# Row norms of a two-layer hybrid diffusion block: 32-column sums of squares, an earlier context norm, a scale built during attention

## The chip, the cores and the metric

The kernel runs on one core of a Trainium2 chip. The metric is the device time of one execution in microseconds (us), lower is better. The engines are named as in the profile: PE (TensorE matmuls) and PEld (its weight loads), DVE (VectorE), ACT (ScalarE), POOL (GpSimd), SP (the queue that issues the DMAs).

## The reference, cut to what matters

Two layers over 512 latent tokens and 256 context tokens, width 1024. Layer 0 is multi-head latent attention, layer 1 a Hyena convolution; each is followed by a gated ConvFFN, and a last RMSNorm ends the program. Every sub-layer starts with a modulated RMSNorm:

```python
def rmsnorm(x, g):
    y = xf * lax.rsqrt(jnp.mean(xf * xf, axis=-1, keepdims=True) + EPS)
    return y * g

mod_x = silu(c) @ mod_w[i] + mod_b[i]          # six vectors of 1024
sh1, sc1, g1, sh2, sc2, g2 = split(mod_x, 6)
hx = rmsnorm(x, norm_mix_g[i]) * (1 + sc1) + sh1
x = x + g1 * mixer(hx)
x = x + g2 * conv_ffn(rmsnorm(x, norm_ffn_g[i]) * (1 + sc2) + sh2)
```

The attention also normalises the 512 query latents (g_q) and the 256 key and value latents (g_kv). Context tokens pass through the same first norm, with their own modulation vector c_ctx, and feed keys and values.

## The kernel before, in words

Activations lie transposed: 128 partitions hold one of 8 chunks of the model width (NC), tokens run along the free axis (T = 512, TC = 256 for the context). Each product is three PE matmuls on a high and a low part (`mm3`, L144); every matmul is recorded on L68. `split_w` (L130) loads a weight block into `wr`, ACT casts it to `wh` (L137), DVE subtracts to `wl` (L138); there are two `wh` and two `wl` buffers.

The stages in order:

- **Filter stage** (`filter_phase`, L383, about 0 to 74 us). Position features give the Hyena filters. In each half `hf`, a loop over four token tiles makes two products `fps`; DVE windows them into `ff` (L439, two buffers), ACT casts to `pqh` (L440), and `pql` is the difference (L441: on POOL for a = 0, on DVE for a = 1). Four small transforms per half follow (`fa`, `fb`, `fo`), whose results DVE combines into `fev` and `fs`. Between the steps `between()` (L506) pops a list of hooks: the modulation rows of layer 0 (`Mods.step_pe`), the squares of x (`nm.add`) and weight splits.
- **Latents** (`latents`, L538, to about 160 us). x is normalised and modulated into `hx` (L314 to L316), products `kv` follow, then the context norm (`rstd_bc`, L306, ordered after the last `hx`), its `ch`/`cl`, the `dq` products, the norm of the key and value latents (`nk`, called halfway through the second `dq` block by `norm_kv`, L570) and that of the query latents (`nq`).
- **Attention** (`attention`, L654, to about 376 us). Eight pairs of heads; each pair has twelve steps, and `side(n, i)` (L848) weaves the next pair's work into step i. Sums of the exponentials go through DRAM (`rst`) and come back as the broadcast `rb`; `normalize` (L813) uses it.
- **Projection and FFN of layer 0** (`project`, L900, to 424 us; `ffn`, L924, to 810 us), then Hyena (to 1020 us), a second projection and FFN, and the final norm.

**A norm** (`Norm`, L240). `add` squares a chunk; all but the last are summed on POOL into `sqa` (L275), the last is squared on DVE into `sq` (L280). `colsum` (L253) then sums over partitions on PE: for each 128 tokens a matmul with the squares as 128x128 stationary operand and one column of ones, so the sums lie along partitions, one column for 128 tokens. `finish` (L284) takes the reciprocal root in eleven DVE instructions on these 2, 4 or 6 columns (L291 to L298), spreads each column over the identity (`dg`, L301) and multiplies by ones into `bc`, the root broadcast over partitions. Norms around `project` and `ffn` work in two token halves (`halves=2`); the first half's `finish` is issued by `mid` in the middle of the last block.

**The scale and shift of FFN 0.** Group (0, 4) of the modulation (1024 columns) is accumulated during `project` by `Mods.step` (L214): eight DMAs of 512 KB and eight DVE instructions into `macc` (L225, L227), then `modp` (ones times `macc`), a copy `ev`, transposes `modq` and the bias add into `modc`; `make_gs` (L236) makes the gain `gsc` that `hx` multiplies by. Group (0, 5) and layer 1's follow inside `ffn`.

The order of instructions on each engine is fixed when the kernel is built, by a scheduler that goes by program order and by when it reckons operands ready, so that work can run ahead of its place in the source (the context's squares, written in `latents`, run at 50 us). `in_order` forces an order of two instructions without a wait.

Of the kernel before, what the change touches and what calls it, by code (L numbers as in the profile page):

```python
# [17 lines left out]
P = 128  # L18
# [29 lines left out]
CST = [("ident", 128), ("perm", 128), ("tneg", 4), ("sgn", 1)]  # L48
# [5 lines left out]
NCST = _o  # L54


@with_exitstack
def hybrid_kernel(ctx, tc, A, out):
# [8 lines left out]
    def mm(*args, **kw):  # L67
        i = nc.tensor.matmul(*args, **kw)  # L68
        in_order(lane["after"], i)
        if lane["since"] is not None:  # L70
            lane["since"].append(i)
        return i
# [24 lines left out]
    cst = gp.tile([P, NCST], F32, name="cst")  # L97
    dma(out=cst, in_=A["cst"])
# [14 lines left out]
    nc.vector.tensor_copy(out=perm_r, in_=K("perm"))  # L113
    ones = gp.tile([P, P], F32, name="ones")
    nc.gpsimd.memset(ones, 1.0)
    modc = gp.tile([P, 2, 48, 2], F32, name="modc")
    gsc = gp.tile([P, 5, 8], F32, name="gsc")
    hcc = gp.tile([P, 3, 24], F32, name="hcc")
    sc = gp.tile([P, 8, 32], F32, name="sc")
    nc.gpsimd.memset(sc, 0.0)  # L120
    act(out=sc[:, :, 0], in_=V("c"), func=AF.Silu)
    act(out=sc[:, :, 1], in_=V("cctx"), func=AF.Silu)
# [36 lines left out]
    class Mods:  # L159
# [11 lines left out]
        def rows(self, lhsT, w, n, first, last):  # L171
            if first:
                self.p = psum[0].tile([P, 512], F32, tag="m", name="modp", bufs=1)
            c = n * 256
            for g in range(4):
                in_order(self.gate, mm(self.p[32 * g:32 * g + 32, :c], lhsT=lhsT, rhs=w[:, g * c:(g + 1) * c], start=first, stop=last))
# [14 lines left out]
        def step_pe(self, n, ws, pool, ahead=0):  # L191
            for _ in range(min(n, len(self.todo))):
                l, u, n, k = self.todo.pop(0)
                self.rows(sc[:, k, :], ws.pop(0), n, k == 0, k == NC - 1)
                if k == NC - 1:
                    self.columns(l, u, n, 2, pool)
                if ahead and len(self.todo) >= ahead:
                    ws.append(self.load(self.todo[ahead - 1], pool, "mw", ahead))

# [14 lines left out]
        def step(self, n, pool, bufs, after):  # L214
# [4 lines left out]
            for _ in range(min(n, len(self.todo))):  # L219
# [3 lines left out]
                if k == 0:  # L223
                    self.acc = pool.tile([P, 2048], F32, tag="macc", name="macc", bufs=2)[:, :n * 1024]
                    i = vts(out=self.acc, in0=w, scalar1=sc[:, k, 0:1], scalar2=None, op0=ALU.mult)  # L225
                else:
                    i = stt(out=self.acc, in0=w, scalar=sc[:, k, 0:1], in1=self.acc, op0=ALU.mult, op1=ALU.add)  # L227
# [12 lines left out]
    class Norm:  # L240
# [7 lines left out]

        def flush(self, lag=0):
# [3 lines left out]
        def colsum(self, src, h, first, last):  # L253
            for t in range(self.nth):
                m = mm(self.cols[h][:, t:t + 1], lhsT=src[:, t * P:(t + 1) * P], rhs=ones[:, 0:1],
                       start=first and t == 0, stop=last and t == self.nth - 1)
                self.last[h] = in_order(self.last[h], m)

        def add(self, xj, h=None):
            self.n_add += 1  # L260
            self.flush(self.nh)
# [9 lines left out]
            sq = self.tmp.tile([P, self.nt * P], F32, tag="sq", name="sq", bufs=2)[:, :w * len(hs)]  # L271
# [12 lines left out]
        def finish(self, bc, h=0, after=None, mm_after=None):  # L284
# [3 lines left out]
            nt, tmp = self.nth, self.tmp  # L288
            v = tmp.tile([P, 3, 8], F32, tag="rsq", name="rsq", bufs=2)
            vv, y, t_ = v[:, 0, :nt], v[:, 1, :nt], v[:, 2, :nt]  # L290
            in_order(after, vts(out=vv, in0=self.cols[h][:, :nt], scalar1=1.0 / self.dim, scalar2=EPS, op0=ALU.mult,  # L291
# [44 lines left out]
    class ToH:  # L336
# [7 lines left out]
        def prep(self, mm_after=None):  # L344
            i = len(self.bc)
            self.bc.append(pso("bc")[:, :self.n])
            self.nm.finish([self.bc[i]], i, None, mm_after)
# [35 lines left out]
    def filter_phase(early, between, mods):  # L383
        with tc.tile_pool(name="fp", bufs=1, side="left", reuse_waits="tile") as fp:
# [42 lines left out]
            for hf in range(2):  # L427
# [3 lines left out]
                for t in range(4):  # L431
                    win = fp.tile([P, 512], F32, tag="win", name="win", bufs=2)
                    act(out=win, in_=dec[:, cs], func=AF.Exp, scale=K("tneg")[:, t:t + 1])
                    for a in range(2):
# [6 lines left out]
                        (vtt if a else nc.gpsimd.tensor_tensor)(out=pq[a][1][:, t, :], in0=f, in1=pq[a][0][:, t, :],  # L441
# [34 lines left out]
    def mla():  # L476
        L = {}
        with ExitStack() as st:
            a1 = st.enter_context(tc.tile_pool(name="a1", bufs=1, side="left"))
            x = a1.tile([P, NC, T], F32, tag="x", name="x")  # L480
            xc = a1.tile([P, NC, TC], F32, tag="xc", name="xc")
            psum_pool(st, "pa", 5)
# [12 lines left out]
            def first_loads():  # L495
# [4 lines left out]
                dma(out=xc, in_=A["ctx"])  # L500

            nm = Norm(NC, 4, D, a1)
            hooks, started, wk = [], [], []
            L["wdkv"] = wk

            def between():  # L506
                if not started:
# [3 lines left out]
                    add = lambda j: (lambda: nm.add(x[:, j, :]))  # L511
                    hooks.extend([()] * 2 + [(step, add(0), add(1))] + [(step, add(j)) for j in range(2, 8)] + [(step, ahead)])
                    hooks[HK] += (lambda: wk.append(split_w(A["wdkv0"], 2048)),)
# [17 lines left out]
            with tc.tile_pool(name="a2", bufs=1, side="left", reuse_waits="tile") as a2:  # L531
                latents(lambda n: mods.step_pe(n, ws, a1, 2), nm, a1, a1, a2, x, xc, L)
# [5 lines left out]
    def latents(step, nm, nrm, a1, a2, x, xc, L):  # L538
# [15 lines left out]
        for rh, rl, n, o in ((hh, hl, T, TC), (ch, cl, TC, 0)):  # L554
# [12 lines left out]
            step(2)  # L567
        nk = Norm(2, 6, 256, nrm)
# [9 lines left out]
        for b in range(2):  # L578
# [40 lines left out]
        kb = L["kb"]  # L619
# [34 lines left out]
    def attention(ab, L):  # L654
# [122 lines left out]
        def value_block(p, kts, sums=None):  # L777
# [20 lines left out]
            if sums is not None:  # L798
# [5 lines left out]
                rs = ab.tile([16, 64], F32, tag="rs", name="rs", bufs=1)  # L804
# [41 lines left out]
        half, parts = {}, []  # L846

# [463 lines left out]
```

## Time and profile before

| | |
|---|---|
| median of 3 runs | 1442.45 us (1441.16 to 1444.59) |
| the profiled execution's own time | 1443.6 us |
| its span in the profile | 1441.8 us |
| PE busy | 1377.4 us (96%) |
| DVE / ACT / POOL busy | 959.4 / 562.4 / 224.9 us |
| mean granted TensorE clock | 0.989 of full speed |

A row of the timeline is: start us, duration us, engine, line, operation, out<-in, shape, count, and in brackets the idle time of the engine before it and what ended it. Merged instructions share a row (x8). f32 matmuls appear as two records each. PEclk is the granted clock as a share of 2.4 GHz. Matmul ends are modelled, so spacing between starts tells more than durations.

### The profile page before, as it was taken

Reading aid. Unit: us, or ns where it says so; the run is one execution under the profiler, and the core shown is the slowest. Engines: PE = TensorE matmul, PEld = TensorE weight load, DVE = VectorE, ACT = ScalarE, POOL = GpSimd, SP = SyncE. Lnnn points to the kernel's source line nnn. Section 1 sums busy time; section 2 is a strip of 40 time slices with the busy share of each in tenths; the row PEclk is TensorE's granted clock in tenths of the full one; section 3 lists DMA queues with packets and bytes.
Section 4 is the critical chain, followed back from the end, with each engine's and each line's share of the span. In section 5 each row is a group of like instructions: output and inputs, shape, how many; then the busy total and the mean of one; then the engine's idle time right before and its main releaser. Section 6 shows DMA issues by size and latency. Waiting matters only on the chain. (4 is left out here: it accounts for less than half of the span.)

```text
span 1441.8 us, 17267 instructions
## 1 busy us (share of the span) xinstructions
PE 1377.4 (96%) x6702; PEld 1088.7 (76%) x6702; DVE 959.4 (67%) x1496; ACT 562.4 (39%) x856; POOL 224.9 (16%) x188
## 2 busy tenths in 40 slices
PE   5899899999989999999999999999999999999997
PEld 2577666665679788787878988787798888888886
DVE  6875766577378777567764788888776553455545
ACT  5434545556335433133432343232344331234320
POOL 3401055354230000000001011332300000000011
PEclk9999999999999999999999999999999999999999
DMA  9672411114362645655513432222313223322121
GB/s 372 220 260 111 139 48 56 44 57 150 106 224 90 240 157 190 244 213 175 183 64 129 172 125 88 97 79 88 128 52 114 83 77 114 113 96 79 60 81 59
DMA packets 46670, 186.58 MB, mean 129 GB/s; under 512 B 5320, under 2 KB 17864, under 8 KB 32380
## 3 DMA queue, kind: packets, MB, share of 16 engines
q1 hardware_dynamic: 46588, 185.48, 37.3%
q8 instruction: 52, 0.85, 0.2%
q14 instruction: 30, 0.25, 0.0%
HBM read 171.29 MB, written 11.60 MB: 127 GB/s over the span
## 5 line engine op out<-in xcount | busy, mean ns | idle before, releaser
L137 ACT CAST wh<-wr 128x1024 fp32r<-128x1024 f32 (+1 forms) x203 | 190.0, 958 | 185.6 <-PE dn L68 89.0
L138 DVE TENSOR_TENSOR wl<-wr,wh 128x1024 fp32r<-128x1024 f32 (+1 forms) x203 | 238.1, 1189 | 18.1 <-ACT wh L137 15.6
L275 POOL TENSOR_TENSOR sqa<-sqa,sq 128x512 f32<-128x512 f32 (+1 forms) x42 | 57.2, 1362 | 844.7 <-ACT sq L273 843.9
L68 PE MATMUL dn<-gh,wl 128*128 128x512 f32 (+1 forms) x396 | 146.7, 370 | 0.0
L68 PE MATMUL dn<-gh,wh 128*128 128x512 f32 (+1 forms) x396 | 146.6, 371 | 0.0
L68 PE MATMUL dn<-gl,wh 128*128 128x512 f32 (+1 forms) x396 | 146.5, 370 | 0.0
L326 DVE SCALAR_TENSOR_TENSOR z<-ua,vec,z 128x511 f32<-128x511 f32 x44 | 33.0, 750 | 111.6 <-ACT z L325 111.5
L970 DVE SCALAR_TENSOR_TENSOR x<-dn,modc,x 128x512 f32<-128x512 f32 (+1 forms) x36 | 24.9, 691 | 109.4 <-PE dn L68 109.4
L325 ACT ACTIVATE z<-ua,vec 128x512 f32<-128x512 f32 x44 | 34.3, 779 | 150.8 <-PE ua L68 150.8
L68 PEld LDWEIGHTS dn<-gh,wh 128*128 128x128 f32 x396 | 74.3, 188 | 15.8 <-ACT wh L137 0.8
L68 PEld LDWEIGHTS dn<-gl,wh 128*128 128x128 f32 x396 | 74.4, 188 | 14.1
L68 PEld LDWEIGHTS dn<-gh,wl 128*128 128x128 f32 x396 | 74.5, 188 | 13.9
L771 POOL TENSOR_TENSOR acc<-acc,pf 128x512 f32<-128x512 f32 x60 | 77.6, 1315 | 26.6 <-ACT pf L761 25.9
L68 PE MATMUL hz<-hyh,wh 128*128 128x512 f32 (+1 forms) x224 | 81.5, 365 | 0.0
L68 PE MATMUL hz<-hyh,wl 128*128 128x512 f32 (+1 forms) x224 | 81.4, 364 | 0.0
L68 PE MATMUL hz<-hyl,wh 128*128 128x512 f32 (+1 forms) x224 | 81.1, 363 | 0.0
L761 ACT ACTIVATE pf<-s 128x512 f32<-128x512 f32 x96 | 57.3, 597 | 45.4 <-PE s L68 42.8
L68 PE MATMUL ua<-hf1h,wh 128*128 128x512 f32 (+1 forms) x192 | 72.9, 380 | 1.1 <-ACT hf1h L315 1.1
L68 PE MATMUL ua<-hf0h,wh 128*128 128x512 f32 (+1 forms) x192 | 73.3, 382 | 0.0
L68 PE MATMUL ua<-hf1l,wh 128*128 128x512 f32 (+1 forms) x192 | 72.8, 379 | 0.5 <-DVE hf1l L316 0.5
L68 PE MATMUL ug<-hf1h,wl 128*128 128x512 f32 (+1 forms) x192 | 73.0, 380 | 0.0
L68 PE MATMUL ua<-hf0l,wh 128*128 128x512 f32 (+1 forms) x192 | 72.9, 380 | 0.0
(382 smaller groups left out, 3383.8 us busy)
## 6 DMA issues: line engine op xcount, KB each, us to landing
wr<-in_wup SPq DMA_DIRECT2D x44, 1024.0 KB
mw<-in_modw SPq DMA_DIRECT2D x40, 1024.0 KB
wr<-in_wdn SPq DMA_DIRECT2D x32, 704.0 KB
wr<-in_win SPq DMA_DIRECT2D x12, 1024.0 KB
mw<-in_modw SPq DMA_DIRECT2D x16, 512.0 KB
fspec<-fs SPq DMA_DIRECT2D x16, 256.0 KB
wr<-in_wo SPq DMA_DIRECT2D x4, 1024.0 KB
fq<-fspec SPq DMA_DIRECT2D x8, 512.0 KB
```

The source lines that it names most:

```text
L68: i = nc.tensor.matmul(*args, **kw)
L137: nc.scalar.copy(out=wh[:, c], in_=wr[:, c])
L138: vtt(out=wl[:, c], in0=wr[:, c], in1=wh[:, c], op=ALU.subtract)
L275: nc.gpsimd.tensor_tensor(out=acc, in0=acc, in1=sq, op=ALU.add)
L325: act(out=z, in_=p, func=AF.Identity, bias=b, scale=w1)
L326: stt(out=z[:, 1:T], in0=p[:, 0:T - 1], scalar=w0, in1=z[:, 1:T], op0=ALU.mult, op1=ALU.add)
L761: act(out=pf, in_=s, func=AF.Exp, scale=ATT_SCALE)
L771: add(out=accs[h], in0=prev, in1=pf, op=ALU.add)
L970: i = stt(out=x[:, q, c], in0=job[0][:, c], scalar=mcol(l, 5, q), in1=x[:, q, c], op0=ALU.mult, op1=ALU.add)
```

## The change

- `colsum` now makes four matmuls with 32 columns of ones as stationary operand and the squares as moving operand, 32*nth tokens each (nth is a half's number of 128-token groups), into four bands of 32 partitions. Each band holds its sums in 32 equal rows. For norms of at most four token groups the sums are issued only in `roots`, the new first part of `finish`.
- The eleven root instructions then work on 128 x (32*nth) elements: 64, 128 or 192 columns. `dg` is gone. The broadcast is four matmuls whose stationary operand `pick` (built once for each pool on POOL) selects one row of a band.
- The roots of x run in a hook of the filter stage; the squares and roots of the context norm move to hooks behind them. In the filter's second half `pql` for a = 1 moves from DVE to POOL.
- `nk` keeps its squares in two tiles; its sums are flushed right after it is filled.
- Group (0, 4) leaves `project`: in attention, pairs 1 to 6, `mod_step` takes a 128x512 slice (16 DMAs of 256 KB into the free `vsb` buffers, 16 DVE instructions), and `mod_rows`/`mod_cols` turn the two halves into `modc` at pairs 4 and 7. `make_gs` then stands before `project`.
- The constant `perm` is loaded later, into a `sq` buffer, and cast on POOL; the exponent-sum tile `rs` shares a tile with `sm`.

```diff
         def colsum(self, src, h, first, last):
-            for t in range(self.nth):
-                m = mm(self.cols[h][:, t:t + 1], lhsT=src[:, t * P:(t + 1) * P], rhs=ones[:, 0:1],
-                       start=first and t == 0, stop=last and t == self.nth - 1)
+            w = self.nth * 32
+            for g in range(4):
+                q = src[g // 2][:, g % 2 * w:(g % 2 + 1) * w] if isinstance(src, list) else src[:, g * w:(g + 1) * w]
+                m = mm(self.cols[h][32 * g:32 * g + 32, :w], lhsT=ones[:, 0:32], rhs=q,
+                       start=first, stop=last)
                 self.last[h] = in_order(self.last[h], m)
...
         def add(self, xj, h=None):
             self.n_add += 1
-            self.flush(self.nh)
+            if self.nt > 4:
+                self.flush(self.nh)
...
-        def finish(self, bc, h=0, after=None, mm_after=None):
+        def roots(self, h=0, after=None, mm_after=None):
...
-            dg = tmp.tile([P, self.nt * P], F32, tag="sq", name="dg", bufs=2)
-            for t in range(nt):
-                vts(out=dg[:, t * P:(t + 1) * P], in0=ident, scalar1=y[:, t:t + 1], scalar2=None, op0=ALU.mult)
-            n = nt * P // len(bc)
-            for i, b in enumerate(bc):
-                in_order(mm_after, mm(b, lhsT=ones, rhs=dg[:, i * n:(i + 1) * n], start=True, stop=True))
+            return y
+
+        def finish(self, bc, h=0, after=None, mm_after=None, y=None):
+            if y is None:
+                y = self.roots(h, after, mm_after)
+            w = self.nth * 32
+            n = 4 // len(bc)
+            for g in range(4):
+                b = bc[g // n][:, (g % n) * w:(g % n + 1) * w]
+                in_order(mm_after, mm(b, lhsT=pick[0][:, g, :], rhs=y, start=True, stop=True))
...
-                        (vtt if a else nc.gpsimd.tensor_tensor)(out=pq[a][1][:, t, :], in0=f, in1=pq[a][0][:, t, :],
+                        (vtt if a and not hf else nc.gpsimd.tensor_tensor)(out=pq[a][1][:, t, :], in0=f, in1=pq[a][0][:, t, :],
                                                             op=ALU.subtract)
...
+                    hooks.append((lambda: L.update(yx=nm.roots(0, None, lane["last"])),))
+                    hooks.extend((lambda j=j: add_ctx(j),) for j in (0, 4))
+                    hooks.extend([(), (), (lambda: L.update(yc=nm_ctx[0].roots(0, None, lane["last"])),)])
...
         to_x = ToH(x, nm, 0, 0, 0, a2, "hx")
+        to_x.prep(None, L["yx"])
         step(2)
         hh, hl = to_x.run()
         bcc = pso("bcc")
-        rstd_bc([xc[:, j, :] for j in range(NC)], 2, D, nrm, [bcc[:, :TC]], to_x.end)
+        nm_ctx.finish([bcc[:, :TC]], 0, None, None, L["yc"])
...
                 for j in range(2):
                     nk.add(ckv[:, j, :])
+                nk.flush()
...
+                    if p and i in (1, 5, 9) and (mod["step"] != NC or p > 3):
+                        mod_step()
+                    if (p, i) in ((4, 0), (7, 0)):
+                        mod_rows(p // 7)
+                    if (p, i) in ((4, 2), (7, 2)):
+                        mod_cols(p // 7)
...
-        mods = Mods([(0, 4, 1)])
+        make_gs(2, 0, 4, "gffn0")
         th = ToH(x, Norm(NC, 4, D, fp, 2), 2, 0, 3, fp, "hf0")
-        project(x, oh, ol, "wo", 0, th.nm, lambda m: (mods.finish(), th.prep(m)), lambda i: mods.step(4, fp, 2, i) if mods.todo else mods.flush())
-        mods.finish()
-        make_gs(2, 0, 4, "gffn0")
+        project(x, oh, ol, "wo", 0, th.nm, th.prep, lambda i: None)
```

## Rows read from the trace of the kernel before

**Rows 1.** The page, part 1: busy time, share of the span, instructions.
```profile
PE 1377.4 (96%) x6702; PEld 1088.7 (76%) x6702; DVE 959.4 (67%) x1496; ACT 562.4 (39%) x856; POOL 224.9 (16%) x188
```

**Rows 2.** Windows: us, PE, PEld, DVE, ACT, POOL busy, PEclk, DMA share, GB/s.
```profile
50.00:60.00 10.00, 7.36 (x32) 5.12 (x30) 7.73 (x21) 4.54 (x12) 4.89 (x6) 1.00 0.35 110
60.00:70.00 10.00, 7.45 (x19) 5.60 (x20) 9.08 (x13) 4.46 (x7) 3.16 (x3) 0.66 0.70 274
```

**Rows 3.** Timeline of the filter's second half.
```profile
54.32 1.28 POOL L441 TENSOR_TENSOR pql<-ff,pqh 128x512 fp32r<-128x512 f32 x1 [1.44 <-ACT pqh L440]
...
59.28 0.72 ACT L273 ACTIVATE sq<-xc 128x256 f32<-128x256 f32 x2 [0.83 <-POOL sqa L275]
...
61.51 1.73 POOL L441 TENSOR_TENSOR pql<-ff,pqh 128x512 fp32r<-128x512 f32 x1
...
63.29 0.79 PE L68 MATMUL fo<-pql,dfto0h 128*128 128x512 f32 x1 [1.99 <-POOL pql L441]
```

**Rows 4.** Timeline of PE in the kv products.
```profile
87.21 0.70 PE L68 MATMUL bcc<-dg,ones 128*128 128x256 f32 x2 [0.78 <-DVE dg L301]
```

**Rows 5.** Timeline of PE in the second dq block.
```profile
127.63 1.39 PE L68 MATMUL cols<-ones,sq 128*128 128x1 f32 x12
...
128.88 0.47 PE L68 MATMUL dq<-hxh,wh 128*128 128x512 f32 x1
...
132.98 1.56 PE L68 MATMUL bk<-dg,ones 128*128 128x384 f32 x4 [1.05 <-DVE dg L301]
```

**Rows 6.** Timeline from the last matmul of project to the first output of FFN 0.
```profile
423.69 0.28 PE L68 MATMUL pj<-oh,wl 128*128 128x256 f32 x1
...
425.84 0.64 PE L68 MATMUL modp<-macc,ones 128*32 128x256 f32 x8 [1.87 <-DVE macc L227]
...
450.31 0.78 ACT L325 ACTIVATE z<-ua,vec 128x512 f32<-128x512 f32 x1 [3.23 <-PE ua L68]
```

**Rows 7.** The same two ends at FFN 1, which has no modulation work.
```profile
1051.65 0.28 PE L68 MATMUL pj<-yh,wl 128*128 128x256 f32 x1
...
1073.52 0.78 ACT L325 ACTIVATE z<-ua,vec 128x512 f32<-128x512 f32 x1 [2.40 <-PE ua L68]
```

**Rows 8.** Timeline of PE, first half of the final norm, inside a running stream.
```profile
1421.81 0.50 PE L68 MATMUL cols<-ones,sqa 128*128 128x1 f32 x4
...
1422.62 0.37 PE L68 MATMUL dn<-gh,wh 128*128 128x256 f32 x1
...
1425.57 0.70 PE L68 MATMUL bc<-dg,ones 128*128 128x256 f32 x2 [0.18 <-DVE dg L301]
1425.91 0.47 PE L68 MATMUL dn<-gh,wh 128*128 128x256 f32 x1
```

**Rows 9.** Lines of DVE by form: busy us, mean ns of one, idle before.
```profile
L314 DVE SCALAR_TENSOR_TENSOR hx<-x,gsc,bc 128x256 f32<-128x256 f32 x48 | 21.7, 476 | 3.8 <-PE bc L68 3.7
...
L301 DVE TENSOR_SCALAR dg<-cst,rsq 128x128 f32<-128x128 f32 x32 | 7.3, 282 | 0.6
...
L296 DVE SCALAR_TENSOR_TENSOR rsq<-rsq 128x2 f32<-128x2 f32 x27 | 4.3, 158 | 0.6
```

**Rows 10.** PE around one 32-column burst in the filter stage (timeline).
```profile
29.75 0.39 PE L68 MATMUL fa<-pql,dfteh 128*128 128x512 f32 x1
29.98 0.40 PE L68 MATMUL fa<-pqh,dftel 128*128 128x512 f32 x1
30.31 1.07 PE L68 MATMUL modp<-mw,sc 128*32 128x512 f32 x8
31.30 0.49 PE L68 MATMUL fb<-pqh,dfteh 128*128 128x512 f32 x1
```

**Rows 11.** Attention: one window, PE's waits (total, times, longest), the macc group.
```profile
200.00:300.00 100.00, 96.73 (x454) 64.81 (x452) 64.39 (x114) 57.51 (x102) 49.31 (x38) 1.00 0.18 54
...
PE mr L68 <- DVE mx L742: 4.3, 6, 1.0
...
L227 DVE SCALAR_TENSOR_TENSOR macc<-mw,sc,macc 128x1024 f32<-128x1024 f32 x14 | 20.8, 1487 | 0.8 <-DMA mw<-in_modw 0.7
```

More of the change, by code (lines that the diff above doesn't have):

```diff
@@ L54 @@
 NCST = _o
+NCP = COFF["perm"][0]
 @with_exitstack
@@ L68, in mm, with tr @@
         i = nc.tensor.matmul(*args, **kw)
+        in_order(lane["after"], i)
+        if lane["since"] is not None:
+            lane["since"].append(i)
+        lane["last"] = i
+        return i
+    def tr(**kw):
+        i = nc.tensor.transpose(**kw)
         in_order(lane["after"], i)
@@ L112, in hybrid_kernel, with make_pick @@
     nc.vector.tensor_copy(out=ident_r, in_=ident)
-    nc.vector.tensor_copy(out=perm_r, in_=K("perm"))
-    ones = gp.tile([P, P], F32, name="ones")
+    ones = gp.tile([P, 64], F32, name="ones")
     nc.gpsimd.memset(ones, 1.0)
+    pick = {}
+    def make_pick(pool):
+        t = pick[0] = pool.tile([P, 4, P], F32, name="pick")
+        nc.gpsimd.memset(t, 0.0)
+        for g in range(4):
+            nc.gpsimd.memset(t[32 * g:32 * g + 1, g, :], 1.0)
     modc = gp.tile([P, 2, 48, 2], F32, name="modc")
@@ L270, in add @@
                 return
-            sq = self.tmp.tile([P, self.nt * P], F32, tag="sq", name="sq", bufs=2)[:, :w * len(hs)]
+            if self.nt > 4:
+                w = self.nt * 64
+                sqs = [self.square("sq")[:, :w] for _ in range(2)]
+                for i, t in enumerate(sqs):
+                    c = slice(i * w, i * w + w)
+                    vtt(out=t, in0=xj[:, c], in1=xj[:, c], op=ALU.mult)
+                self.due.append((self.n_add, sqs, 0, j == 0, j == n - 1))
+                return
+            sq = self.square("sq")[:, :w * len(hs)]
             if j < n - 1 and n > 2:
@@ L481, in mla @@
             xc = a1.tile([P, NC, TC], F32, tag="xc", name="xc")
+            s2 = pick[1] = a1.tile([P, 8, 32], F32, name="s2")
+            nc.gpsimd.memset(s2, 0.0)
+            act(out=s2[:, :, 0], in_=V("c"), func=AF.Silu)
+            act(out=s2[:, :, 1], in_=V("cctx"), func=AF.Silu)
+            nc.gpsimd.tensor_copy(out=sc, in_=s2[:, :, 0])
+            make_pick(a1)
             psum_pool(st, "pa", 5)
@@ L500, in first_loads @@
                 dma(out=xc, in_=A["ctx"])
+                perm = a1.tile([P, T], F32, tag="sq", name="perm", bufs=2)[:, :P]
+                dma(out=perm, in_=A["cst"][:, NCP:])
+                nc.gpsimd.tensor_copy(out=perm_r, in_=perm)
             nm = Norm(NC, 4, D, a1)
+            nm_ctx = []
             hooks, started, wk = [], [], []
@@ L846, in attention, with mod_load, mod_step, mod_rows @@
         half, parts = {}, []
+        mod = {"step": 0}
+        def mod_load(n):
+            hf, k = divmod(n, NC)
+            w = mod[n] = at.tile([P, T], F32, tag="vsb", name="mw", bufs=2)
+            dma(out=w, in_=A["modw"][0, k * P:(k + 1) * P, 4096 + hf * 512:4608 + hf * 512])
+        def mod_step():
+            n = mod["step"]
+            if n >= 2 * NC:
+                return
+            mod["step"] = n + 1
+            hf, k = divmod(n, NC)
+            w = mod.pop(n)
+            if k == 0:
+                acc = mod["acc"] = ab.tile([P, T], F32, tag="macc", name="macc", bufs=1)
+                vts(out=acc, in0=w, scalar1=sc[:, k:k + 1], scalar2=None, op0=ALU.mult)
+            else:
+                acc = mod["acc"]
+                stt(out=acc, in0=w, scalar=sc[:, k:k + 1], in1=acc, op0=ALU.mult, op1=ALU.add)
+            if n + 2 < 2 * NC:
+                mod_load(n + 2)
+        def mod_rows(hf):
+            mp = pst("modp")[:, :P]
+            for g in range(4):
+                mm(mp[32 * g:32 * g + 32], lhsT=ones[:, 0:32], rhs=mod["acc"][:, g * P:(g + 1) * P], start=True, stop=True)
+            mod["ev"] = ab.tile([P, T], F32, tag="rb", name="ev", bufs=1)[:, :P]
+            nc.scalar.copy(out=mod["ev"], in_=mp)
+        def mod_cols(hf):
+            q = pst("modq")[:, :P]
+            tr(out=q, in_=mod.pop("ev"), identity=ident)
+            c = slice(32 + 4 * hf, 36 + 4 * hf)
+            vtt(out=modc[:, 0, c, 0], in0=q.rearrange("p (g r) -> p g r", r=32)[:, :, 0], in1=V("modb0", 32 + 4 * hf, 36 + 4 * hf),
+                op=ALU.add)
+        for n in range(2):
+            mod_load(n)
         def side(n, i):
```

57 lines of the change are left out of this document (35 added, 22 removed).

## The prediction

> **What bounds the kernel now.** I read the page's shares first. PE is busy 1377.4 us of the span, 96%, and DVE 959.4 [rows 1], so a norm that gets cheaper on another engine is worth only the stretch in which PE waits for it. The windows then show where PE has gaps: in attention 200 to 300 holds 96.73 of 100 [rows 11], but 50 to 60 holds 7.36 of 10 and 60 to 70 holds 7.45 [rows 2]. In 60 to 70 the granted clock is 0.66 of 2.4 GHz, so part of that stretch ran at the 1.2 GHz level after a stretch in which PE had idled: 10 x 0.34 = 3.4 us of full-speed time are missing there, beside the idle time. I therefore read the timeline at the joins of the stages, each for what PE waits for last. In the filter's second half it is `pql` on POOL, 1.99 us ahead of `fo`; ACT comes to it late, since squares of the context stand in its queue and wait for POOL [rows 3]. In the kv products it is `dg` of the context norm, 0.78 us [rows 4]; in the dq products the sums of `nk`, 127.63 to 128.88, and 1.05 us on its `dg` [rows 5]. Between `project` and FFN 0 it is `macc` on DVE, 1.87 us, and then more: last `pj` to first `z` takes 450.31 - 423.69 = 26.62 us [rows 6], and the same two ends are 1073.52 - 1051.65 = 21.87 us apart at FFN 1, which has no modulation there [rows 7]. The norm halves that end inside a running stream show little: eight sum records take 1422.62 - 1421.81 = 0.81 us, and `bc` takes 0.34 and waits 0.18 [rows 8].
>
> **Time base.** The profiled execution took 1443.6 us (span 1441.8 and 1.8 around it), 1.15 over the median. The sum is made against 1443.6 and then lowered by 1.15. Two in a thousand, 2.9 us, is about what a measurement of this kernel can tell from no change: faster means under 1439.6, slower over 1445.3.
>
> **Prices.** Three recur. A burst of 32-column matmuls: eight records of 512 columns take 31.30 - 30.31 = 0.99 us [rows 10], so 0.99 x columns / 512, plus 0.10 for entering it (the product ahead of it takes 30.31 - 29.98 = 0.33, the one before that 0.23). A record with a stationary operand of its own: 0.81 / 8 = 0.10 [rows 8]. A wider root instruction: 476 ns at 256 columns [rows 9] against 158 at 2 [rows 9] gives (476 - 158) / 254 = 1.25 ns a column, so 0.08 us more at 64 columns, 0.16 at 128 and 0.24 at 192; eleven make a chain 0.9, 1.8 or 2.6 us longer, and each `dg` that goes gives 0.28 back.
>
> **A. Filter, second half: -1.0.** The context squares leave ACT's queue ahead of `pqh`, which could give PE's 1.99 us back and part of the 3.4 us. But DVE is busy 9.08 of 10 in 60 to 70 and 7.73 in 50 to 60 [rows 2]; where it sets the pace, no more than its idle time, 0.92 + 2.27 = 3.2 us, can go. Four `pql` leave DVE, two root chains come onto it (x and the context, 128 and 64 columns). POOL gets four more `pql`; alone one takes 1.28 us, and 1.73 where it follows another [rows 3]; POOL is busy 4.89 and 3.16 there [rows 2], so there is room in sum, though each lies between two steps of the chain. The bounds are -3.2 and 4 x 1.28 = +5.1. I take -1.0, nearer the gain, since the `fo` wait is on the path and the room is seen.
>
> A rule bears on that: the Trainium skill, page "SBUF — State Buffer", section "Who interferes with whom", has DVE and GpSimd share one port pair as an exclusive lock, taken also by a DVE operation with two SBUF inputs against GpSimd's reads. The rows agree in direction (1.73 beside 1.28); by the rule alone POOL's eight would each be the longer one.
>
> **B. Context norm in kv: -0.8.** Its roots are ready before `kv` begins, and the 0.78 us wait goes [rows 4]. Bounds -1.2 and 0.
>
> **C. `nk` and `nq`: -2.2.** The sums of `nk` come twice, 12 records and 1.25 us each time [rows 5]; after, 192 columns cost 0.37 + 0.10, so 2 x (1.25 - 0.47) = -1.6. The wait of 1.05 on `dg` goes, as the sums are flushed early. The sums of `nq`, 16 records at 0.10, become two bursts of 128 columns: 1.6 - (2 x 0.25 + 0.1) = -1.0; its chain is 1.8 longer less four `dg` of 0.28, about +0.5, since what follows waits for it. The chain of `nk` is 2.6 longer less six `dg`, +0.9, which the early flush hides or not; I charge it. -1.6 - 1.05 - 1.0 + 0.5 + 0.9 = -2.2, bounds -3.7 and 0 (a later root chain on DVE could take it all).
>
> **D. Joining FFN 0: -4.2.** With no modulation left there the join becomes that of FFN 1: 21.87 - 26.62 = -4.75 [rows 6, 7], and this norm's halves cost 2 x 0.3 more (as under F). The smallest gain is the 1.87 us of the `macc` wait, the largest adds a rest of 1.4 for the eight `macc` of 1.49 us [rows 11] that leave DVE: bounds -6.2 and -1.9. Late next is the last half's root chain. Eight DMAs of 512 KB leave SP's queue here.
>
> **E. Attention: +1.2.** PE gets 8 records of 128 columns (0.25), the entry, and a transpose, some 0.5 us twice, in a stretch where it is busy 96.73 of 100 [rows 11], so +1.0. DVE gets 16 instructions of half 1.487 us, 11.9 in all, at 64.39% busy [rows 11]; they are hidden if they fall in its gaps, and PE already waits 4.3 us in 6 places for DVE's `mx` [rows 11]. SP gets 16 DMAs, each issued only after the DVE step two before has freed its buffer, with the loads of values and the exponent sums queued behind. `ev` takes the buffer of `rb`, so its ACT copy can wait for `normalize`, with ACT's later exponentials behind it. I put 0.2 on all that; the bounds are +0.5 and doubled `mx` waits, 4.3 + 1.0 = +5.3.
>
> **F. The other six norm halves: +2.1.** Per half, 16 records become two bursts of 64 columns at 0.12 each plus the entry; between that 0.34 and the old 0.81 I take 0.6 (-0.2). `bc` becomes eight records, at most 0.10 each by stationary loads, against 0.34: +0.5. That is +0.3 for five. The last half lies on the tail, where the chain counts too: +0.3 + 0.9 - two `dg`, 0.56 = +0.6. Sum 2.1, bounds -1.0 (`bc` stays at 0.34, its 0.18 wait goes) and 3.5.
>
> Costed at nothing: `pick` and its memsets (POOL is busy 16% [rows 1]; without that cover `bc` would wait some us once a pool), the late `perm` (hidden unless its cast holds a `sq` buffer when the squares want it), `rs` inside `sm`.
>
> **Sum.** -1.0 - 0.8 - 2.2 - 4.2 + 1.2 + 2.1 = -4.9, so 1438.7 for the profiled execution and 1437.5 for the median.
>
> **Rivals.**
> **POOL becomes the bound in the filter.** The four moved `pql` stand between `pqh` and `fo`; POOL also sums squares there and casts `perm`. For it: POOL is already `fo`'s releaser [rows 3]. Against: its room. If all four come onto the path, A is +5.1 and another stretch like 60 to 70 at the lower clock adds 3.4, so 1437.5 + 1.0 + 8.5 = 1447.0. It decides when `fo` gets its last `pql` over 3.4 us later than at 63.29. Chance 0.14; slower.
> **FFN 0 gains only its wait.** The change does not do what it says: the halves' sums already stood at the end [rows 8], and after the `macc` wait the split of weights or the last root chain holds PE. D is -1.9, the time 1439.8. For it: DVE is the releaser at this join too. Against: FFN 1's 21.87 [rows 7]. Chance 0.13; same.
> **Each burst stalls PE.** If the whole 0.33 ahead of a burst were idle instead of 0.10, about 15 bursts (eight halves, two of `nk`, `nq`, x, context, two in attention) cost 15 x 0.23 = 3.5 more: 1441.0. Rows 10 show a gap of 0.10 at the one place read, so 0.05; same. The Trainium skill, page "TensorEngine Tiling (Array Packing)", section "Key Properties", says that changing the tiling mode drains the TensorE, which speaks for this rival; the row's 0.10 agrees in sign and is small.
> **All joins give their most.** A -3.2 and D -6.2 make 1433.3, chance 0.10; faster.
>
> **How the numbers follow.** The forecast has 0.58, with its own range 1430.5 to 1439.6. Faster is 0.58 + 0.10 = 0.68, same 0.13 + 0.05 = 0.18, slower 0.14. The range goes down to 1430 (the full gains of A and D, with F at its lower bound) and up to 1445, which holds both "same" rivals and leaves out most of the POOL case.
>
> **What would show it.** A: `fo` starts before 63.3 and the clock in 60 to 70 is above 0.66; wrong if `fo` still waits for POOL, longer. B and C: no wait of `bcc` or `bk` on DVE. D: last `pj` to first `z` near 22. E: `mr` waits on `mx` stay near 4.3. F: `bc` records spaced by 0.10 or less, the sum bursts about 0.6. The whole is wrong if attention lengthens by over 4 us or FFN 0's join stays above 25.

## The result and the profile after

The changed kernel takes 1457.91 us (median of 4 runs, 1454.54 to 1461.23) against 1443.52 for the kernel before (median of 4): a ratio of 1.010 with a 95% interval of 1.0082 to 1.0118. It is 14.4 us slower; 1437.5 had been forecast, and the range ended at 1445. Its profiled execution took 1461.23 us with a span of 1459.3, so the two profiles lie 17.5 us apart. Every distance below is read from one profiled execution of a kernel; times are medians.

The stages as distances between the starts of named matmuls, in us, for the two kernels:

| from, to | before | after | difference |
|---|---|---|---|
| start, last `fps` (filter, second half) | 53.82 | 67.08 | +13.26 |
| last `fps`, first `kv` | 20.79 | 25.04 | +4.25 |
| first `kv`, first `pk` (latents) | 62.57 | 56.81 | -5.76 |
| first `pk`, first `pj` (attention) | 239.02 | 249.39 | +10.37 |
| first, last `pj` (project) | 47.49 | 47.08 | -0.41 |
| last `pj`, first `ua` (join of FFN 0) | 7.46 | 1.71 | -5.75 |
| first `ua`, end | 1010.65 | 1012.19 | +1.54 |

The latents and the join gained about what was hoped for or more; the filter and attention lost 28 us. PE is hardly busier than before: 1380.1 us against 1377.4 [rows 1].

**The filter.** The windows of the changed kernel (columns as in [rows 2]) show a stretch with no matmul at all, and a mean granted clock of 0.64 and 0.68 in and behind it, between the two levels of 0.5 and 1; the third line lies in attention.

```profile
50.00:60.00 10.00, 0.00 (x0) 0.00 (x0) 0.69 (x1) 3.12 (x6) 8.52 (x8) 0.64 0.84 315
60.00:70.00 10.00, 8.81 (x41) 6.29 (x41) 6.70 (x10) 4.55 (x8) 5.22 (x4) 0.68 0.00 1
...
210.00:220.00 10.00, 6.24 (x20) 3.90 (x20) 6.48 (x13) 3.45 (x7) 1.26 (x1) 0.66 0.39 115
```

The timeline of the changed kernel around the hole, first ACT, then POOL, then PE:

```profile
48.85 0.72 ACT L469 ACTIVATE win<-dec,cst 128x512 f32<-128x512 f32 x1
49.48 0.61 ACT L304 ACTIVATE sq<-x 128x512 f32<-128x512 f32 x1
51.55 0.63 ACT L304 ACTIVATE sq<-x 128x512 f32<-128x512 f32 x1 [1.46 <-POOL sqa L306]
...
60.08 0.58 ACT L196 COPY ev<-modp 128x512 f32<-128x512 f32 x1 [2.55 <-POOL sqa L306]
...
53.46 0.29 POOL L545 CAST perm_r<-perm 128x128 fp32r<-128x128 f32 x1
54.25 5.79 POOL L306 TENSOR_TENSOR sqa<-sqa,sq 128x512 f32<-128x512 f32 x4 [0.51 <-ACT sq L304]
...
60.72 1.11 PE L199 MATMUL modq<-cst,ev 128*128 128x128 f32 x4 [12.15 <-ACT ev L196]
```

And the same squares and the same copy in the timeline of ACT in the kernel before:

```profile
32.16 0.63 ACT L273 ACTIVATE sq<-x 128x512 f32<-128x512 f32 x1
...
40.32 0.64 ACT L273 ACTIVATE sq<-x 128x512 f32<-128x512 f32 x1 [1.06 <-POOL sqa L275]
...
50.14 0.58 ACT L181 COPY ev<-modp 128x512 f32<-128x512 f32 x1
```

The squares of x have moved from 32 to 41 us, between the filter's casts, to 49 to 58, behind them all. There they run one at a time: most wait until POOL has summed the one before. The copy `ev` of the modulation rows stands behind them in ACT's queue; its own tile comes from the same two `sq` buffers, and it waits another 2.55 us for POOL's last addition. PE waits 12.15 us for it. So inside the hole POOL's additions set the pace. That the hole is there at all is a matter of order: the first square starts right behind `win`, the instruction ahead of it, so it did not wait for a buffer on the chip; it was put there when the kernel was built.

**Attention.** The whole stretch from first `pk` to first `pj` as one window, before and after (columns as in [rows 2]):

```profile
137.20:376.20 239.00, 226.21 (x1044) 153.16 (x1042) 154.75 (x276) 132.69 (x233) 100.75 (x78) 0.99 0.24 76
...
148.90:398.30 249.40, 232.00 (x1067) 155.71 (x1065) 167.52 (x288) 132.78 (x234) 103.09 (x83) 0.97 0.29 89
```

PE's idle time grows from 12.8 to 17.4 us, which is 4.6 of the 10.4. Its busy time grows by 5.8 us, with 23 more records and a mean granted clock of 0.97 instead of 0.99. PE's waits in the changed kernel from 185 to 400 (total, times, longest):

```profile
PE mr L69 <- DVE mx L800: 5.5, 7, 1.2
PE rot L69 <- DVE rpl L699: 2.8, 1, 2.8
PE sm L69 <- DVE m L797: 1.5, 1, 1.5
...
PE modq L77 <- ACT ev L933: 1.4, 1, 1.4
```

The long one in the timeline, POOL first, then DVE, then PE:

```profile
197.11 5.00 POOL L829 TENSOR_TENSOR acc<-acc,pf 128x512 f32<-128x512 f32 x4
...
198.87 3.79 DVE L924 SCALAR_TENSOR_TENSOR macc<-mw,sc,macc 128x512 f32<-128x512 f32 x1
...
211.18 0.88 DVE L924 SCALAR_TENSOR_TENSOR macc<-mw,sc,macc 128x512 f32<-128x512 f32 x1 [0.91 <-DMA mw<-in_modw]
...
212.45 0.68 DVE L699 TENSOR_TENSOR rpl<-pq,rph 128x512 fp32r<-128x512 f32 x1
...
213.18 0.79 PE L69 MATMUL rot<-rpl,perm_r 128*128 128x512 f32 x1 [2.82 <-DVE rpl L699]
```

Sums written for pairs 1 to 3 stand between 193 and 215 us: they ran ahead of their places, wait for their DMAs, and the rope product `rpl` stands behind them. After PE's wait the clock of 210 to 220 is 0.66. One sum takes 3.79 us; it ends just behind four POOL additions in a row.

**The join and the norm halves.** Timeline of the changed kernel; compare [rows 6] and [rows 8]:

```profile
445.40 0.28 PE L69 MATMUL pj<-oh,wl 128*128 128x256 f32 x1
...
447.11 0.38 PE L69 MATMUL ua<-hf0h,wh 128*128 128x256 f32 x1
...
467.25 0.78 ACT L361 ACTIVATE z<-ua,vec 128x512 f32<-128x512 f32 x1 [4.25 <-PE ua L69]
...
1438.23 0.28 PE L69 MATMUL dn<-gh,wl 128*128 128x256 f32 x1
1438.43 0.32 PE L69 MATMUL cols<-sqa,ones 128*32 128x64 f32 x8
1438.57 0.30 PE L69 MATMUL cols<-sq,ones 128*32 128x64 f32 x8
1438.80 0.39 PE L69 MATMUL dn<-gh,wh 128*128 128x256 f32 x1
...
1442.11 1.10 PE L69 MATMUL bc<-rsq,pick 128*128 128x64 f32 x8
1443.03 0.36 PE L69 MATMUL dn<-gh,wl 128*128 128x256 f32 x1
```

Last `pj` to first `z` is 467.25 - 445.40 = 21.85 us, the 22 that was foretold (20.0 to 22.0 in the runs below in which this join has no modulation work). A half's sums take 0.37 us (0.81 before), its broadcast 0.92 (0.34 before).

### The profile page after: what moved, and what is told of

The parts are those of the page before. It is cut to its first block, busy times and chain, and to the rows that moved or that the text cites. A ratio compares the mean times of both kernels' runs of the same rounds, so it can differ in the third digit from the quotient of the medians.

```text
span 1459.3 us, 17570 instructions
## 1 busy us (share of the span) xinstructions
PE 1380.1 (95%) x6844; PEld 1086.0 (74%) x6844; DVE 963.8 (66%) x1470; ACT 562.8 (39%) x857; POOL 231.0 (16%) x209
## 5 line engine op out<-in xcount | busy, mean ns | idle before, releaser
L306 POOL TENSOR_TENSOR sqa<-sqa,sq 128x512 f32<-128x512 f32 (+1 forms) x42 | 53.7, 1277 | 836.2 <-ACT sq L304 803.0
L69 PE MATMUL ug<-hf0h,wl 128*128 128x512 f32 (+1 forms) x192 | 72.7, 379 | 0.0
```

What stands on the lines that cost most here:

```text
L306: nc.gpsimd.tensor_tensor(out=acc, in0=acc, in1=sq, op=ALU.add)
```

## The experiments

Distances of the runs on which the argument rests most, worked out as in the table above:

| run | median, us | last `fps` | to `kv` | to `pk` | to `pj` | join | `ua` to end |
|---|---|---|---|---|---|---|---|
| e1 `perm` apart | 1449.78 | 54.06 | 25.56 | 59.81 | 248.18 | 1.70 | 1008.42 |
| e2 scale in `project` | 1458.10 | 67.03 | 25.04 | 57.10 | 237.33 | 11.03 | 1011.36 |
| e3 ordered sums | 1459.54 | 67.60 | 25.02 | 56.81 | 251.03 | 1.71 | 1007.49 |
| e5 context norm back | 1445.44 | 54.50 | 22.39 | 61.26 | 248.53 | 1.70 | 1010.63 |
| e6 `pql` back | 1446.27 | 54.44 | 25.77 | 60.15 | 248.21 | 1.71 | 1012.03 |
| e7 norm alone | 1444.11 | 54.06 | 22.36 | 60.70 | 237.74 | 10.92 | 1007.91 |
| e8 sums in dq | 1438.66 | 53.88 | 22.38 | 67.16 | 237.45 | 1.70 | 1010.28 |
| r9 one column | 1441.00 | 54.32 | 22.39 | 61.78 | 242.64 | 1.71 | 1008.60 |
| r11 `perm` in before | 1463.18 | 66.84 | 27.88 | 59.89 | 239.09 | 7.46 | 1013.48 |

The last column holds nearly the same code in most runs and still spreads by 6 us from one execution to the next; the readings rest on the other columns and the medians.

**e1, `perm` in a tile of its own.**

```diff
-                perm = a1.tile([P, T], F32, tag="sq", name="perm", bufs=2)[:, :P]
+                perm = a1.tile([P, P], F32, name="perm")
```

> Edit: the late load of `perm` gets a tile of its own (512 bytes a partition) instead of one of the two `sq` buffers; nothing else. Theory P (the `perm` buffer): until the cast of `perm` has run, the squares of x have one buffer fewer, so they were put behind the filter's casts in ACT's queue and the copy of the modulation rows stood behind them; with the buffer free the 12.15 us wait of PE for that copy goes, the last `fps` starts near 54 instead of 67, `kv` starts near 76 instead of 92, and the time falls by 11 to 15 us, to 1443 to 1447. Rival Q (POOL's four more `pql`): POOL is the bound there whatever the buffers, PE still waits over 6 us in 45 to 65, and the time stays over 1452.

The ratio to before is 1.0043 (1.0026 to 1.0061). The squares are back between the casts and the last `fps` starts at 54.06: theory P holds, with 8.1 us at the medians of the expected 11 to 15. In the profiles 13.0 us are gone at the last `fps`, 12.5 at the first `kv`, which starts at 79.62 instead of the expected 76, and 9.5 at the first `pk`, as the latents are 3.0 longer than in the changed kernel. The ten runs of e1 spread by 11.3 us, and the profiled one (1446.84) lies 2.9 under their median, that of the changed kernel 3.3 over its own. Timeline of this run (POOL, DVE, ACT, PE):

```profile
53.13 2.56 POOL L477 TENSOR_TENSOR pql<-ff,pqh 128x512 fp32r<-128x512 f32 x2 [2.45 <-ACT pqh L476]
...
53.34 1.18 DVE L325 TENSOR_SCALAR rsq<-rsq 128x128 int32<-128x128 int32 x1
54.55 1.29 DVE L328 SCALAR_TENSOR_TENSOR rsq<-rsq 128x128 f32<-128x128 f32 x1
...
67.85 0.28 DVE L329 TENSOR_TENSOR rsq<-rsq 128x128 f32<-128x128 f32 x1
...
64.11 1.98 ACT L150 CAST wh<-wr 128x1024 fp32r<-128x1024 f32 x2
...
66.63 0.50 PE L69 MATMUL fo<-pqh,dfto1h 128*128 128x512 f32 x1 [2.44 <-ACT fee L489]
...
77.10 1.94 PE L69 MATMUL bcc<-rsq,pick 128*128 128x64 f32 x8 [5.04 <-DVE rsq L330]
...
79.62 0.79 PE L69 MATMUL kv<-hxh,wh 128*128 128x512 f32 x1 [0.58 <-ACT hxh L351]
```

The broadcast of the context's roots now stands on PE ahead of `kv` and waits 5.04 us for a chain on DVE that stands ahead of the first `hx`. Before that PE waits 2.44 us for `fee`, which stands behind the weight casts on ACT. And a root instruction of 128 columns takes 1.2 to 1.3 us while POOL's `pql` runs, 0.28 when POOL is idle.

**r11, the same from the other side: the kernel before with only the late `perm`.**

```diff
+                perm = a1.tile([P, T], F32, tag="sq", name="perm", bufs=2)[:, :P]
+                dma(out=perm, in_=A["cst"][:, NCP:])
+                nc.gpsimd.tensor_copy(out=perm_r, in_=perm)
...
```

> Edit of the kernel before, alone: `perm` is loaded late into a `sq` buffer and cast on POOL, as in the change. Theory P: the last `fps` starts near 67 instead of 53.8, as in the changed kernel; half 2 then runs without part of its old waits, so the time rises by 7 to 13 us, to 1450 to 1457. Rival P2 (the hole needs the change's other moves, four more `pql` on POOL above all): under 1447.

1.0135 (1.0121 to 1.0149): this one edit costs 19.5 us, more than the whole change. P2 falls; the hole needs neither the extra `pql` on POOL nor the early context norm. The last `fps` is where it was foretold (66.84); the size was foretold too small, as the way from there to `kv` is 7.1 us longer than before instead of shorter. PE's waits from 45 to 95 us:

```profile
PE cols L69 <- POOL sqa L275: 14.8, 2, 11.6
PE bc L69 <- DVE dg L301: 2.5, 1, 2.5
PE modp L69 <- DMA mw<-in_modw: 2.4, 1, 2.4
```

The 11.6 are the hole: here the old norm's sums of x stand first behind it and wait for POOL's additions directly. The other 3.2 (sums of the context), the `dg` and the modulation slice come between 80 and 91 us; the kernel before has no such waits ahead of `kv`.

**e2, group (0, 4) back in `project`.** The load, the steps, `mod_rows` and `mod_cols` leave attention:

```diff
+        mods = Mods([(0, 4, 1)])
...
+        project(x, oh, ol, "wo", 0, th.nm, lambda m: (mods.finish(), th.prep(m)), lambda i: mods.step(4, fp, 2, i) if mods.todo else mods.flush())
+        mods.finish()
         make_gs(2, 0, 4, "gffn0")
...
-        project(x, oh, ol, "wo", 0, th.nm, th.prep, lambda i: None)
```

> Edit: group (0, 4) goes back from attention into `project`, as in the kernel before; the rest of the change stays. Theory A (the sums in attention cost more than the join gains): first `pk` to first `pj` takes 239 us as before instead of 249.4, last `pj` to first `z` of FFN 0 is back at 26 to 27 from 21, and the time falls by 10.5 - 5.8 = 4 to 5 us, to 1452.5 to 1454.5. Rival B (attention is longer for another reason, as the shared tile of `sm` and `rs` or the squares of `nk`): `pk` to `pj` stays over 246 and the time rises by about 5 us, to 1463.

Attention is at once back at 237.33, so theory A holds there and rival B falls: the move costs it 12 us. The time does not fall (1.0104, 1.0089 to 1.0119), as the join, which was to return to that of the kernel before, takes 11.03 us. Its rows on PE:

```profile
435.65 0.64 PE L69 MATMUL modp<-macc,ones 128*32 128x256 f32 x8 [1.86 <-DVE macc L244]
...
441.48 1.94 PE L69 MATMUL bc<-rsq,pick 128*128 128x64 f32 x8 [4.22 <-DVE rsq L330]
```

So with the new norm, this join would be 3.6 us worse than before, and the move gains 9.3 there and gives back 12.

**e3, the sums held at their places.**

```diff
-                nc.vector.reduce_max(out=m2s[h][:, qt, i:i + 1], in_=sm, axis=AX.X)
+                mod["dve"] = nc.vector.reduce_max(out=m2s[h][:, qt, i:i + 1], in_=sm, axis=AX.X)
...
+            in_order(mod["dve"], m)
```

> Edit: each of the 16 DVE sums in attention is ordered after the latest maximum written ahead of it, so it keeps the place it has in the source; nothing waits. Theory A1 (the sums ran ahead: eight of them stand in DVE's queue within the first pair, each waiting for its DMA with the rope products behind it): the 2.82 us wait of `rot` and the low clock behind it go, `pk` to `pj` falls from 249.4 to 241 to 244, and the time falls by 5 to 8 us, to 1450 to 1453. Rival A2 (the work and the DMAs themselves cost, wherever they stand): `pk` to `pj` stays within 2 us of 249.4 and the time within 3 us of 1458.

A1 falls: 1.0113 (1.0098 to 1.0128), attention even 1.6 us longer. The `rot` wait is gone; in its place PE's wait for the maxima is twice the 5.5 us of the changed kernel. The lengths are those that A2 foretold. The view of the group `macc` (min, median, max ns) says why; this is e3:

```profile
PE mr L69 <- DVE mx L800: 10.7, 7, 2.7
...
L924 DVE SCALAR_TENSOR_TENSOR macc<-mw,sc,macc x14: 786/1112/1768, 227.2 to 367.0; 128x512 f32<-128x512 f32 x14
```

Spread over attention, a sum of 0.75 us lies beside POOL's additions of the exponentials and takes 1.11 in the median, on an engine whose maxima PE waits for.

**e4, e1 and e3 together.**

> Edit: the tile of its own for `perm` and the ordered sums together. If P and A1 hold and are independent, the gains add: 18 +- 3 us below the changed kernel, 1437 to 1443, which is 1 to 6 us under the kernel before and near the forecast of 1437.5. If one of them only uncovers another wait, the sum falls short by over 4 us. Rival Q and A2: over 1450.

1452.5 us, 1.0064 (1.0048 to 1.0081): with A1 gone there is nothing to add.

**r9, 14 sums on one column.** On top of e5 below:

```diff
-                stt(out=acc, in0=w, scalar=sc[:, k:k + 1], in1=acc, op0=ALU.mult, op1=ALU.add)
+                stt(out=acc[:, 0:1], in0=w[:, 0:1], scalar=sc[:, k:k + 1], in1=acc[:, 0:1], op0=ALU.mult, op1=ALU.add)
```

> Edit, on top of the run with the context norm back: 14 of the 16 sums in attention work on one column of 512 (the rest of the modulation vector is left out); DMAs, order, rows and columns stay. Theory A5 (the DVE time of the sums is the price): first `s` to first `pj` falls from 207.5 to 197 to 201 (the rows on PE and the copy's wait are left, 1 to 4 us over 196.7), time 1435 to 1439 from 1445.4. Rival A6 (the DMAs, each ahead of its sum on DVE, or the rows are the price): it stays over 204, time over 1443.

Between the two: first `s` to first `pj` is 203.15, 4.3 us under e5's 207.45 and 6.5 over the 196.66 of e7, which has no sums there; the time is 4.4 us under e5's. What the edit takes out is some 40% of the price. The rest is left with nearly empty sums, and the profile shows where: DVE still waits for its slices, with `rpl` behind them, and a sum of one column can still take 3.28 us: it runs from 186.86 to 190.14, beside four additions of POOL that end at 190.12. So the run does not part the DVE time of the sums cleanly from the rest. The group of the sums (min, median, max ns) and the timeline:

```profile
L922 DVE SCALAR_TENSOR_TENSOR macc<-mw,sc,macc x14: 202/219/3279, 186.9 to 300.9; 128x1 f32<-128x1 f32 x14
...
198.40 0.66 DVE L922 SCALAR_TENSOR_TENSOR macc<-mw,sc,macc 128x1 f32<-128x1 f32 x1 [1.21 <-DMA mw<-in_modw]
...
200.17 0.50 PE L69 MATMUL rot<-rpl,perm_r 128*128 128x512 f32 x1 [2.52 <-DVE rpl L697]
```

**e5, the context norm back in `latents`.** On top of e1:

```diff
-                    hooks.extend((lambda j=j: add_ctx(j),) for j in (0, 4))
-                    hooks.extend([(), (), (lambda: L.update(yc=nm_ctx[0].roots(0, None, lane["last"])),)])
...
-        nm_ctx.finish([bcc[:, :TC]], 0, None, None, L["yc"])
+        rstd_bc([xc[:, j, :] for j in range(NC)], 2, D, nrm, [bcc[:, :TC]], to_x.end)
```

> Edit, on top of the tile of its own for `perm`: the context norm's squares and roots go back into `latents`, behind the last `hx`, as in the kernel before. Theory C (the early context norm is what delays `kv` there): in the run with `perm` apart PE stands 2.44 us for `fee`, whose ACT turn is behind context squares and a weight cast, and 5.04 us for the context's roots, which stand on DVE ahead of `hx`; both go, `kv` starts between 71.5 and 74.6 us instead of 79.6, a wait of about 1 us for the context's roots comes back inside `kv`, and the time falls by 4 to 8 us from 1449.8, to 1442 to 1446. Rival C2 (the roots of x beside POOL's `pql` are what delays: 1.0 to 1.3 us for one of 128 columns there against 0.28 elsewhere): `kv` still starts after 78 and the time stays over 1447.

1.0011 (0.9993 to 1.0028), 4.3 us under e1. `kv` starts at 76.89, 2.7 earlier, and the latents give 1.45 back: theory C has the sign, and for `kv` not the whole size (71.5 to 74.6 was expected). The profiles show 1.3 us of gain up to the first `pk`; where the rest of the 4.3 comes from they do not show. The `fee` wait stays (2.5 us): the squares, written later now, run ahead into the filter all the same and stand on ACT where they stood, with the weight casts between them and `fee`. What moved back is the root chain and its broadcast. Against the kernel before, `kv` is still 2.3 us late.

**e6, `pql` back on DVE, context norm early.** On top of e1:

```diff
-                        (vtt if a and not hf else nc.gpsimd.tensor_tensor)(out=pq[a][1][:, t, :], in0=f, in1=pq[a][0][:, t, :],
+                        (vtt if a else nc.gpsimd.tensor_tensor)(out=pq[a][1][:, t, :], in0=f, in1=pq[a][0][:, t, :],
```

> Edit, on top of the tile of its own for `perm`: the second half's `pql` for a = 1 goes back from POOL to DVE; the context norm stays early. Theory C: the bound of this stretch is the context norm, so `kv` starts within 1.5 us of 79.6 and the time is within 3 us of 1449.8. Rival C2: with half as many `pql` on POOL the roots of x on DVE are shorter and `kv` starts by 3 us or more earlier, time under 1446.5.

`kv` starts at 80.21, as theory C says and not by 3 us earlier, as C2 says. The time is 1.0023 (1.0004 to 1.0043), 3.5 us under e1's median: outside theory C's 3 us, and by 0.2 us inside what C2 gave. No stage up to FFN 0 explains it, and the ten runs of each of the two kernels spread by 11.3 and 10.6 us. This run does not settle whether the move of `pql` costs something; it does settle that it isn't what holds `kv`.

**e7, the new norm alone** (the edits of e1, e2, e5 and e6).

> Edit: only the new norm (32-column sums, wide roots, `pick` broadcast, the early flush of `nk`) stays; the context norm is back in `latents`, `pql` on DVE, group (0, 4) in `project`, `perm` in a tile of its own. The prediction's terms C (-2.2), F (+2.1) and a wider chain at FFN 0's join (+0.6; the run with the scale back in `project` showed 11.0 us from last `pj` to first `ua` against 7.5, so up to +3.6): within 4 us of the kernel before, 1441 to 1446.5. Rival (the new norm itself carries the loss, through its root chains of 64 to 192 columns on DVE): over 1449.

1.0008 (0.9994 to 1.0021): the new norm by itself changes nothing that can be measured. It gains 1.87 us in the latents (60.70 against 62.57) and 1.28 in attention, and loses 1.57 between last `fps` and `kv` and 3.46 at the join. Ahead of `kv` PE waits 4.9 us there for `fev` on DVE, in whose queue the 128-column roots of x and a weight split now stand; what share the roots have in it was not tested.

**r10, e7 with the sums issued as they come.**

```diff
-            if self.nt > 4:
-                self.flush(self.nh)
+            self.flush(self.nh)
```

> Edit, on top of the norm alone: `add` flushes the sums as they come for every norm, as in the kernel before, not only in `roots`. Theory J (issued at the norm's end the sums of the first half stand behind the modulation rows on PE, so its root chain starts after them): last `pj` to first `ua` of FFN 0 falls from 10.9 to 7.5 to 8.5 us, time 1440 to 1442.5 from 1444.1. Rival J2 (the wider chain of eleven roots is what makes this join longer): it stays over 10 and the time within 1.5 us of 1444.

1.0000 (0.9991 to 1.0009), join 10.93: theory J falls. The sums were not late to begin with: in e7 they stand 4.0 us ahead of the last `pj`, as they do here, so that at this join the edit changes nothing. What is late is the chain. One row of e7, two of this run, and one of the kernel before, where the last sums start at 419.69:

```profile
417.87 0.32 PE L69 MATMUL cols<-sq,ones 128*32 128x64 f32 x8
...
418.34 0.32 PE L69 MATMUL cols<-sq,ones 128*32 128x64 f32 x8
...
425.39 0.22 DVE L322 TENSOR_SCALAR rsq<-cols 128x64 f32<-128x64 f32 x1
...
420.23 0.16 DVE L291 TENSOR_SCALAR rsq<-cols 128x2 f32<-128x2 f32 x1 [1.39 <-PE cols L68]
```

The first root instruction stands on DVE 7 us behind the sums, behind two `macc` and a weight split, where in the kernel before it stood 0.5 us behind. J2 foretold the numbers, but not for its reason: most instructions of the chain are only 0.07 us longer here (0.23 against 0.16), while the chain begins 6.5 us later behind its sums. Why it is ordered there stays open.

**e8, the sums in the dq products.** On top of e5; the 16 sums, DMAs, rows and columns stand in the loop over the dq blocks:

```diff
+            in_order(cend, m)
...
         for b in range(2):
+            for _ in range(NC):
+                mod_step()
...
+            mod_rows(b)
+            mod_cols(b)
```

> Edit, on top of the run with the context norm back: the 16 sums of group (0, 4), their DMAs, rows and columns go from attention into the dq products, where DVE is less busy (1.85 to 5.84 of 10 in 100 to 130 before), ordered after the last `cl`. Theory A3 (in attention the sums cost because DVE is on the path there: PE's wait for `mx` doubles when they keep their places): `pk` to `pj` is back at 238 to 240 us, the wait for `mx` at 5 us, last `pj` to first `ua` stays at 1.7, the dq products grow by 0 to 2, and the time falls by 7 to 10 us against the run beside it, to 1433 to 1438, under the kernel before. Rival A4 (their price comes along wherever they stand, as DMAs on SP's queue or rows on PE): the time stays within 3 us of the run beside it.

1438.66 us, 0.9969 (0.9957 to 0.9982): 5 us faster than the kernel before, 19 faster than the changed one and 6.8 faster than e5, just under the 7 to 10 expected. The stage distances of its profiled execution, one of its slower runs, show 1.9 of the 5. Attention is back at 237.45, the join stays at 1.70: theory A3 holds and A4 falls. The latents pay 5.9, more than the 0 to 2 expected, and PE's waits there and in attention show what for, the root broadcast `bcc` of the context among it:

```profile
PE mr L69 <- DVE mx L843: 5.1, 7, 1.0
...
PE bcc L69 <- DVE rsq L330: 1.4, 1, 1.4
PE modp L69 <- DVE macc L653: 1.4, 1, 1.4
PE modq L77 <- ACT ev L663: 1.4, 2, 1.0
```

**r12, e8 with early sums and later rows.** The sums as in r10; `mod_rows` and `mod_cols` of the halves stand behind the second dq block and behind the squares of `nq`.

> Edit, on top of the run with the sums in dq: sums of the norms issued as they come, and the rows and columns of the two modulation halves put later, behind the second dq block and behind the sums of `nq`. In the run with the sums in dq PE waits 1.4 us for `macc` and 1.4 us for its copy; by theory both go, and the time falls from 1438.7 by 1 to 3 us, to 1435.5 to 1437.5. Rival: DVE is then late for the roots of `nk` and `nq` and the time stays within 1 us of 1438.7.

A miss: 1442.84 us (0.9995, 0.9984 to 1.0005), with first `kv` to first `pk` at 69.19. PE waits 3.0 us for the copy, now in one place, and 2.1 us in the sums of `nq` for POOL's `sqa`, a wait that e8 does not have. Which of the two edits lost how much was not separated; e8 remains the best.

## Why the prediction was wrong

- **Costed at nothing, and the largest loss: the late `perm`.** The prediction said "hidden unless its cast holds a `sq` buffer when the squares want it", put no price on the condition and did not look whether it held. It held: e1 takes 8.1 us of the 14.4 away, r11 makes 19.5 us with that edit alone. The prediction looked for a wait at the buffer; what cost was the order: with one buffer of two taken until a cast whose DMA is issued last, the squares were put behind the half's casts, and the copy for PE, which needs such a buffer too, behind the squares. That the buffer is the cause e1 and r11 show; by which rule the scheduler then chose this order is not shown.
- **E, attention: +1.2 forecast, bounds +0.5 to +5.3, measured +10.4.** The step priced PE's rows; its upper bound was doubled `mx` waits, which come in e3 (10.7) and not in the changed kernel (5.5). It left out that the sums can run ahead of their places and hold DVE at a DMA (2.8 us of `rot`, and the low clock behind it), and that a sum is longer beside POOL. The copy `ev`, named and put into the 0.2, made PE wait 1.4 us. The queue behind the waiting instruction, `rpl` on DVE, was not named. Idle time is 4.6 us of the loss; the other 5.8 are busy time of PE, most of it by the lower mean clock (an estimate: 0.02 of 232 us are 4.6).
- **B, context norm: -0.8 forecast.** The wait in `kv` did go, and 1.45 us with it (e1 against e5), but the chain moved ahead of `hx`, on the path: 3.2 us between last `fps` and `kv` (25.56 against 22.39). A wait of the same chain stood in a worse place.
- **A, filter: -1.0 forecast; the gain is not there even without the hole.** With `perm` apart and the context norm back (e5), `kv` still starts at 76.89 instead of 74.61, and with `pql` back on DVE as well (e7) at 76.42. Why was not separated. The rival in which POOL becomes the bound had the sign and the stage, and inside the hole it is POOL's additions, which it names, that ACT waits for. But its cause, the four moved `pql`, is not what e1, e6 and r11 show, and 1447.0 was far from enough.
- **C and D were right.** The latents gain 1.87 us with the norm alone (e7; -2.2). Last `pj` to first `z` is 21.85, a gain of 4.77 (-4.2). For D there is luck in it: with the new norm and the modulation still in `project` the same two ends are 30.58 us apart (e2), a loss of 4 that no term has and that the move hid.
- **F was near in its prices.** `bc` takes 0.92 (0.84 by the step), the sums 0.37 (the step took 0.6), so a half in the stream costs about 0.1 instead of 0.3; last `dn` to the end is 13.44 instead of 12.26, +1.2 (+0.6), and between 12.6 and 13.4 in the other runs with the new norm. The norm alone is within the measurement of no change.
- **The stall by bursts** falls: the two bursts of a half put 1438.80 - 1438.23 - 0.12 = 0.45 us into the stream altogether (0.12 is the spacing of `dn` records there). Less the 2 x 0.12 of the step, 0.21 are left for entering and leaving both, where this rival had 0.33 for each. The Trainium skill, page "TensorEngine Tiling (Array Packing)", section "Key Properties", has a drain at each change of the tiling mode; this bounds what two changes cost here.

## What to carry to other kernels

A buffer lent to a rare tile is part of the schedule: look who else takes from that ring while it is lent, and build the order before pricing the move at nothing. Work moved under an engine's idle time needs a place where nothing on the path stands behind it in the same queue: the same sums cost 10 us in attention and 6 among the dq products. A move of a small chain is priced where it lands, by what stands behind it, not by the wait that it leaves.

## What the runs showed of the hardware

DVE instructions with their operands in SBUF stretch to POOL's instruction beside them: 1.18 and 1.29 us beside `pql` of 1.28 against 0.28 alone (e1), and up to 3.79 beside four additions in a row. The width of the instruction matters little: a sum of one column took 3.28 us beside four additions in r9, against 0.22 in the median. DVE instructions that read one operand from PSUM kept their time (`ff` at 55.76 and 58.52 us of e1, 0.68 beside POOL's additions). The Trainium skill, page "SBUF — State Buffer", section "Who interferes with whom", calls the port pair of the two an exclusive lock; these rows agree.

How far a kernel's runs spread differs: ten runs of e1 lie between 1444.58 us (mean granted clock 0.988) and 1455.88 (0.978), where r10's ten lie within 2.1 us. In e1 the longer runs are those with the lower mean clock. What makes one kernel spread more than another no run here shows: r11, the slowest of all, has its four runs within 3.3 us.
